# Three full-attention heads first in an encoder's attention stage, with queries loaded in token halves

## The chip, the cores and the metric

The kernel runs on one core of a Trainium2 chip. The core has a matrix engine (PE, with its weight loads shown as PEld), a vector engine (DVE), a scalar engine for pointwise functions (ACT), a second elementwise engine (POOL) and SP, which here only issues transfers. The metric is the device time of one execution in microseconds (us). Before the change it is 2045.96 us, the median of 3 runs (2044.32 to 2046.07).

## The reference

The model is a trunk of four residual layers over 1024 tokens of width 1024, all in float32: attention, MLP, spatial gating, MLP, then a final norm. The change touches the attention layer alone:

```
proj = rmsnorm(x) @ w_in                     # q, k, v of both groups in one projection
qa, ka, va, qb, kb, vb = split(proj)         # 8 query heads and 2 key heads in each group, 64 wide
qa, ka = rope(qa), rope(ka)
oa = window_attention(qa, ka, va, sink)      # group A: keys at most 128 tokens away, and a sink logit
qb, kb = rope(rmsnorm(qb)), rope(rmsnorm(kb))
ob = softmax(qb kb^T / 8) vb                 # group B: all 1024 keys
x = x + concat(oa, ob) @ w_out
```

A banded head (letter a) needs the scores of some 3 of 8 key blocks for each query block; an unbanded head (letter b) needs all of them. Both subtract the row maximum before the exponential.

## The kernel before, in words

Numbers are kept accurate by splitting each operand into a high and a low part, so that most products are three matmuls (`mm3`). The weights are split by ACT and DVE (a few by POOL) ahead of use, in the order of a list (`items`, `ahead`).

**The projections.** The attention layer begins with three of them. The first gives k and v. The second (`lin` with `evac_qb`) gives the queries of the b heads, the third (`lin` with `evac_qa`) those of the a heads. Each `lin` runs over two halves of 512 tokens; in a half it holds four PSUM banks (of 8 in all, `psp`) and goes through eight steps k of 12 matmuls. After each step it calls a hook, if there is one, and `tick()`, which moves every waiting `chain` on by one `yield`. At the end of a half, `rotate` reads two banks at a time: four DVE operations, two POOL operations, and later, in its chain, a norm (b heads and keys), a split and a store of the rotated queries to DRAM (`qs`). Only then is `ready[key, half]` set.

**The heads.** All 16 heads run in the order of the string at L538, "bbaababababababa". `load_head` (L561) reads a head's queries back from DRAM into R1 (high part, twice) and R2 (low part in its lower 64 partitions), three transfers on SP's queue for all 1024 tokens. `load_k` does the same for the keys of a key head and sets a constant with a memset on POOL. `mx_units` gives the work on the row maxima: 16 units for a b head, each one matmul over 512 keys and one DVE reduction out of PSUM (L614); 8 units for an a head (L598). Four query blocks on, `bcast` turns the maxima into a row of R2. For the first two heads this is done with four small matmuls (tile bc) and a DVE copy (L640), for all others through DRAM: a transpose on DVE and two transfers (tile md).

`st_units` gives the score units. In a b head each of 16 units is two matmuls (st), an exponential and a cast on ACT (`exps_b`, L660 and L663), and a subtraction for the low part on POOL or DVE (L665; DVE does five of the first ten, then one in eight). The product with the values (`av`, three matmuls for each unit) is held back by six units (`LAG`). `finish_head` normalises two heads of a kind at a time.

**The order around the change.** The loop over heads at L811 issues a unit of scores, then as many maxima of the heads to come as its goal asks for, then an av that is six units old, then a `tick()`. The goal of head n is all maxima of heads up to n + 1 and 0.6 of those of head n + 2. Before the loop, `qa_hook` (L800) loads the first two b heads in step 1 of the second half of the third projection and issues 20 of their 32 maxima in steps 3 to 7. The program's order is a priority: an instruction whose buffer is not free can be placed behind others when the kernel is built. On the chip each engine then works in its fixed order. The attention stage is followed by the output projection (`out_proj`), which takes the last av units along.

The large buffers are 44 blocks (`blkp`) that weights, rotated queries, R1, R2, keys and the outputs of the exponentials share.

Of the kernel before, what the change touches and what calls it, by code (L numbers as in the profile page):

```python
# [10 lines left out]
ALU = mybir.AluOpType  # L11
# [4 lines left out]
T = 1024  # L16
KT = D // P
HN = 512
# [14 lines left out]
def tile_kernel(ctx: ExitStack, tc: tile.TileContext, I, out, upto=99, dbg=None):  # L33
    nc = tc.nc
    pe, act, dve, pool, sp = nc.tensor, nc.scalar, nc.vector, nc.gpsimd, nc.sync
# [11 lines left out]
    def nm(s):  # L47
        uid[0] += 1
        return f"{s}_{uid[0]}"

    def blk(s, dt=F32R):
        return blkp.tile([P, 2, HN], dt, tag="blk", name=nm(s))
# [13 lines left out]
    def f(ap):  # L66
        return ap.bitcast(F32)
# [202 lines left out]
    def lin(rhs, evac, spare=1, swap=False, hook=None, run=True):  # L270


        g = gi[0]
        gi[0] += 1
        for half in range(2):
            acc = [ps("lin") for _ in range(4)]
            for k in range(KT):
                w = wt(g, k)
                r = rhs(k, half)
                for m in range(4):  # L280
                    ls = slice(m * P, (m + 1) * P)
                    if swap:
                        mm3(acc[m], r, w, ls, k == 0, k == KT - 1)
                    else:
                        mm3(acc[m], w, r, ls, k == 0, k == KT - 1)
                if run and k == 1:
                    ahead(base[g] + 4 + spare)
                if run and half == 1 and k % 2 == 1:
                    ahead(base[g] + 4 + spare + (k + 1) // 2)
                if hook is not None:  # L290
                    hook(half, k)
                tick()
            for m in range(4):
                evac(m, half, acc[m])
# [72 lines left out]
    h = {}  # L367
# [30 lines left out]
    def table(name):  # L398
        t = blk("tab", F32)
        sp.dma_start(t, I[name].rearrange("p (h t) -> p h t", h=2))  # L400
        return t

    rst = {}
# [18 lines left out]
    ready = {}  # L422

    def rotate(key, half, p1, p2, C, S, c1=None, c2=None, late=0):


        de, w1, w2 = blk("de", F32), tr("w1"), tr("w2")
        for o, p_, c, t in ((w1, p2, c2, S), (de[:, 0], p1, c1, C), (w2, p1, c1, S), (de[:, 1], p2, c2, C)):
            if c is None:
                dve.tensor_tensor(o, p_, t, op=ALU.mult)  # L430
            else:
                dve.scalar_tensor_tensor(o, p_, c, t, op0=ALU.mult, op1=ALU.mult)
        if c1 is not None:
            s1, s2 = tr("s1"), tr("s2")
            act.activation(s1, p1, AF.Square)
            act.activation(s2, p2, AF.Square)
            pool.tensor_tensor(s1, s1, s2, op=ALU.add)
        pool.tensor_tensor(de[:, 0], de[:, 0], w1, op=ALU.subtract)
        pool.tensor_tensor(de[:, 1], de[:, 1], w2, op=ALU.add)

        def chain():
            for _ in range(1 + late):
                yield 1
            if c1 is not None:
                yield 1
                s = ps("hss")
                mm(s, blk32, s1, True, True)
                yield 1
                y0, a, q = tr("hy"), tr("ha"), tr("hq")

                dve.scalar_tensor_tensor(a, s, 1.0 / 64.0, evb[:, half], op0=ALU.mult, op1=ALU.add)
                act.activation(y0, a, AF.Ln)
                act.activation(y0, y0, AF.Exp, scale=-0.5)
                act.activation(q, y0, AF.Square)
                yield 1
                newton(y0, q, a, 1.0, a)
                if key == "k":
                    act.copy(a[0:64], rst[half][0:64])
                for i in range(2):
                    dve.tensor_tensor(de[:, i], de[:, i], a, op=ALU.mult)  # L460
            yield 1
            for i in range(2):
                q = blk("qh")
                split(q, de[:, i])
                sp.dma_start(qs[key][:, :, :, i, half * HN : (half + 1) * HN].rearrange("a j r t -> (j r) a t"), f(q))
            ready[key, half] = True

        chains.append(chain())
# [4 lines left out]
    for half in range(2):  # L473
# [27 lines left out]
        for tb in range(4):  # L501
            sc = rc[:, tb : tb + 1]
            for kv in range(4):
                src = vp[tb // 2][:, tb % 2, kv * 64 : (kv + 1) * 64]
                hi = v1[kv][:, half * 4 + tb, 0:64]
# [13 lines left out]
    pend = {}  # L519
# [3 lines left out]
        if m % 2 == 1:  # L523
            rotate(f"b{m // 2}", half, pend[m - 1], pend[m], bc_[:, half], bs_[:, half], col(C_QN1), col(C_QN2), m // 2)

    lin(lambda k, half: h[k, half], evac_qb)
    ac, as_ = table("tac"), table("tas")
    for half in range(2):
        dve.tensor_tensor(ac[:, half], ac[:, half], rst[half], op=ALU.mult)
        dve.tensor_tensor(as_[:, half], as_[:, half], rst[half], op=ALU.mult)  # L530

    def evac_qa(m, half, p_):
        pend[m] = p_
        if m % 2 == 1:
            rotate(f"a{m // 2}", half, pend[m - 1], pend[m], ac[:, half], as_[:, half])


    heads, seen = [], {"a": 0, "b": 0}  # L538
    for c in "bbaababababababa":
        heads.append((c, seen[c]))  # L540
        seen[c] += 1
    k1, k2 = {}, {}
    R1, R2 = {}, {}
# [6 lines left out]
    def load_k(kv):  # L550
        a = blk("k1")
        b = blk("k2")
        hi, lo = (qs["k"][part, kv].rearrange("r n t -> (r n) t") for part in range(2))
        sp.dma_start(f(a[0:64].rearrange("p a b -> p (a b)")), hi)
        sp.dma_start(f(a[64:128].rearrange("p a b -> p (a b)")), lo)
        sp.dma_start(f(b[0:64].rearrange("p a b -> p (a b)")), hi)
        pool.memset(f(b[64:128]), -1.0 / 64.0)
        k1[kv] = a.rearrange("p a b -> p (a b)")
        k2[kv] = b.rearrange("p a b -> p (a b)")

    def load_head(n):  # L561
        hd = heads[n]
        kv = kv_of(hd)
        if kv not in k1:
            load_k(kv)
        key = f"{hd[0]}{hd[1] // 4}"
        assert all((q, half) in ready for q in (key, "k") for half in range(2))
        hi, lo = (qs[key][part, hd[1] % 4].rearrange("r n t -> (r n) t") for part in range(2))
        a, b = blk("r1"), blk("r2")
        a = a.rearrange("p a b -> p (a b)")  # L570
        b = b.rearrange("p a b -> p (a b)")
        sp.dma_start(f(a[0:64]), hi)
        sp.dma_start(f(a[64:128]), hi)
        sp.dma_start(f(b[0:64]), lo)
        R1[n], R2[n] = a, b

    md = drp.tile([16, 2, 32 * P], F32, tag="md", name="md")

# [42 lines left out]

    def bcast(n, half, m4):
        r2 = R2[n][64:128, half * HN : (half + 1) * HN]
        if n > 1:

            t = smp.tile([P, 32], F32, tag="m4", name=nm("mt"))
            dve.transpose(t, f(m4))
            yield 1
            sp.dma_start(md[n, half].rearrange("(a b i) -> b a i", a=32, b=4), t)
            for _ in range(3):  # L630
                yield 1
            sp.dma_start(f(r2), md[n, half, 0:HN].partition_broadcast(64))
            shifted.add((n, half))
            return
        for _ in range(2):
            yield 1
        p_ = ps("bc")
        for i in range(4):
            mm(p_[:, i * P : (i + 1) * P], m4[:, i : i + 1].to_broadcast([P, P]), ident, i == 0, i == 3)
        dve.tensor_copy(r2, p_[64:128])  # L640
        shifted.add((n, half))
# [135 lines left out]
    avq = []  # L777
    LAG = 6
    loaded = [0]
    mxq = []  # L780
    mxn = [0, 0]

    def load_to(n):
        while loaded[0] < min(n, 16):
            load_head(loaded[0])
            loaded[0] += 1

    def n_mx(n):
        return sum(8 if hd[0] == "a" else 16 for hd in heads[: max(n, 0)])

    def mx_to(count):

        while mxn[1] < min(count, n_mx(16)):
            if not mxq:
                mxq.extend(mx_units(mxn[0]))
                mxn[0] += 1
            mxq.pop(0)()
            mxn[1] += 1

    def qa_hook(half, k):  # L800
        if half == 1:
            if k == 1:
                load_to(2)
            if k >= 3:
                mx_to((k - 3 + 1) * 4)

    lin(lambda k, half: h[k, half], evac_qa, run=False, hook=qa_hook)
    h.clear()
# [2 lines left out]
    for n in range(16):  # L811
        if n > 0:
            load_to(n + 3)
        units = st_units(n)
        start, goal = mxn[1], n_mx(n + 2) + int((n_mx(n + 3) - n_mx(n + 2)) * 0.6)
        if n == 0:
            goal = n_mx(2)
        for i, u in enumerate(units):
            avs = u()
            mx_to(start + -(-(goal - start) * (i + 1) // len(units)))  # L820
            avq.append(avs)
            if len(avq) > LAG:
                for a in avq.pop(0):
                    a()
            tick()
        if n >= 13:
            ahead(base[3] + (n - 12))
# [579 lines left out]
```

## Time and profile before

| | us |
|---|---|
| median of 3 runs | 2045.96 |
| profiled execution, own time | 2044.68 |
| its span, first to last instruction | 2042.9 |
| PE busy | 2007.8 (98%) |
| DVE busy | 1402.2 (69%) |
| ACT busy | 982.4 (48%) |
| POOL busy | 591.3 (29%) |

Times in the views are us from the start of the span; 1.78 us of the execution's own time lie outside the span. [...] A row of a timeline gives start, duration, engine, line, operation, tiles and shape, the count of merged instructions and, in brackets, the engine's idle time before it and what ended that. A row of groups gives line, engine, operation, tiles, shapes and count, then busy time and mean ns, then idle time before and its releasers. All matmuls have one line (L72), so they are told apart by tile. Matmuls are pipelined: one is shown as 389 ns long while the next begins much earlier, so that short gaps do not show as idle time.

### The profile page before, as it was taken

The numbers are of one execution on the slowest core, as the hardware profiler recorded it, in microseconds if no ns is written. First come the engines' busy times: TensorE is split into PE (matmuls) and PEld (weight loads), VectorE is DVE, ScalarE is ACT, GpSimd is POOL, SyncE is SP. The second block draws the span as 40 slices with busy tenths as digits, with TensorE's granted clock in tenths as the row PEclk, the third lists the DMA queues.
The fourth block names the chain that finished last, engine by engine and source line by source line (L and its number), as shares of the span: only waits on it lengthen the run. The fifth ranks groups of instructions, "written<-read, shape, count | busy, mean of one in ns | idle before, by whom it ended". The sixth has DMA issues, their size and how long they took to land.

```text
span 2042.9 us, 27046 instructions
## 1 busy us (share of the span) xinstructions
PE 2007.8 (98%) x9038; PEld 1653.3 (81%) x9038; DVE 1402.2 (69%) x2281; ACT 982.4 (48%) x1822; POOL 591.3 (29%) x460
## 2 busy tenths in 40 slices
PE   8998999999999999999999999999999999999998
PEld 7786777778788888888888888888788888888886
DVE  6677867745886666856797445555976667836976
ACT  5526779873543333444454434433533333544443
POOL 5535557543142222100102126332232223000113
PEclk9999999999999999999999999999999999999999
DMA  5463242245054444848464210432254445856443
GB/s 172 139 191 94 65 114 57 57 135 167 36 177 149 160 149 162 295 162 314 131 215 145 78 57 11 145 119 98 88 179 146 150 159 206 300 210 208 160 134 124
DMA packets 213244, 299.05 MB, mean 146 GB/s; under 512 B 23792, under 2 KB 92912, under 8 KB 213104
## 3 DMA queue, kind: packets, MB, share of 16 engines
q1 hardware_dynamic: 213104, 297.32, 43.9%
q8 instruction: 71, 1.16, 0.2%
q14 instruction: 69, 0.57, 0.1%
HBM read 210.80 MB, written 86.44 MB: 145 GB/s over the span
## 4 chain that ended last, share of the span: by engine, by line
PE 82%; DVE 7%; ACT 5%; issue 3%; POOL 1%; DMA 1%; DVEq 0%; ACTq 0%; SPq 0%; POOLq 0%
PE up L72 27%; PE lin L72 17%; PE dy L72 17%; PE dx L72 13%; PE av L72 2%; PE st L72 2%; PE vp L72 1%; ACT pe L660 1%; PE kp L72 1%; ACT pp L663 1%; PE mx L72 1%; DVE w L145 1%; DVE mb L614 1%; DVE o L712 1%; PE dz L72 1%
## 5 line engine op out<-in xcount | busy, mean ns | idle before, releaser
L72 PE MATMUL up<-h,w 128*128 128x512 f32 x1536 | 363.2, 389 | 1.0 <-ACT w L144 0.6
L72 PE MATMUL dy<-w,w 128*128 128x512 f32 x1488 | 353.8, 389 | 0.0
L72 PEld LDWEIGHTS up<-h,w 128*128 128x128 f32 x1536 | 288.1, 188 | 61.8 <-ACT w L144 1.0
L72 PEld LDWEIGHTS dy<-w,w 128*128 128x128 f32 x1488 | 279.3, 188 | 58.4 <-ACT w L144 0.2
L313 POOL TENSOR_TENSOR ss<-ss,sq 128x512 f32<-128x512 f32 x69 | 105.9, 1536 | 653.7 <-ACT sq L311 556.3
L72 PE MATMUL dx<-w,w 128*128 128x512 f32 x1152 | 276.7, 389 | 0.0
L72 PE MATMUL up<-w,w 128*128 128x512 f32 x1152 | 276.7, 390 | 0.0
L72 PEld LDWEIGHTS up<-w,w 128*128 128x128 f32 x1152 | 216.3, 188 | 45.7 <-ACT h L863 0.5
L72 PEld LDWEIGHTS dx<-w,w 128*128 128x128 f32 x1152 | 216.3, 188 | 44.8
L144 ACT CAST w<-wr 128x512 fp32r<-128x512 f32 x288 | 167.6, 620 | 142.0 <-DVE wr L177 36.3
L145 DVE TENSOR_TENSOR w<-wr,w 128x512 fp32r<-128x512 f32 x288 | 200.9, 707 | 22.6 <-ACT w L144 18.5
L72 PE MATMUL lin<-h,w 128*128 128x512 f32 x768 | 180.8, 393 | 0.3 <-ACT mixl L1231 0.3
L984 POOL TENSOR_TENSOR t<-ua,ub 128x512 f32<-128x512 f32 x32 | 44.6, 1394 | 448.8 <-ACT ua L931 427.3
L72 PEld LDWEIGHTS lin<-h,w 128*128 128x128 f32 x768 | 143.4, 188 | 32.2 <-issue 2.4
L145 DVE TENSOR_TENSOR w<-ur,w 128x512 fp32r<-128x512 f32 x224 | 158.4, 717 | 5.8 <-ACT w L144 5.7
L665 POOL TENSOR_TENSOR pp<-pe,pp 128x512 fp32r<-128x512 f32 x107 | 140.9, 1338 | 73.1 <-ACT pp L663 48.6
L144 ACT CAST w<-ur 128x512 fp32r<-128x512 f32 x224 | 135.9, 620 | 42.9 <-DVE w L145 21.6
L145 DVE TENSOR_TENSOR w<-ws,w 128x512 fp32r<-128x512 f32 x128 | 94.9, 741 | 66.9 <-ACT w L144 66.3
L72 PE MATMUL st<-r,k 128*128 128x512 f32 (+2 forms) x384 | 130.3, 405 | 5.3 <-DVE mb L614 2.4
L144 ACT CAST w<-ws 128x512 fp32r<-128x512 f32 x128 | 79.4, 620 | 110.0 <-DVE ws L224 75.2
L931 ACT ACTIVATE ua<-ua 128x512 f32<-128x512 f32 x64 | 40.5, 633 | 168.9 <-DVE ua L930 168.7
L72 PE MATMUL av<-pp,v 128*128 128x512 f32 x384 | 110.4, 399 | 5.3 <-DVE mb L614 2.9
(195 smaller groups left out, 3012.5 us busy)
## 6 DMA issues: line engine op xcount, KB each, us to landing
ur<-ucd SPq DMA_DIRECT2D x224, 256.0 KB
wr<-in_w SPq DMA_DIRECT2D x256, 128.0 KB
ucd<-t SPq DMA_DIRECT2D x128, 256.0 KB
wr<-in_w SPq DMA_DIRECT2D x128, 256.0 KB
ucd<-ub SPq DMA_DIRECT2D x64, 256.0 KB
x<-in_xT SPq DMA_DIRECT2D x32, 256.0 KB
xmd<-x SPq DMA_DIRECT2D x32, 256.0 KB
ucd<-ua SPq DMA_DIRECT2D x32, 256.0 KB
```

The costliest lines, as they stand in the source:

```text
L72: last_mm[0] = pe.matmul(o, l, r, start=start, stop=stop, **kw)
L144: act.copy(w[:, 0], src)
L145: dve.tensor_tensor(w[:, 1], src, f(w[:, 0]), op=ALU.subtract)
L313: pool.tensor_tensor(acc, acc, t, op=ALU.add)
L614: dve.tensor_reduce(M[n][:, tb, kh : kh + 1], p_, axis=AX.X, op=ALU.max)
L660: act.activation(e, p_, AF.Exp, scale=0.125)
L663: act.copy(pp[:, 0], e)
L665: lo.tensor_tensor(pp[:, 1], e, f(pp[:, 0]), op=ALU.subtract)
L712: dve.tensor_tensor(out_, out_, y, op=ALU.mult)
L931: act.activation(dst, dst, AF.Square)
L984: pool.tensor_tensor(t3, ua[:, 1], ub[:, 1], op=ALU.subtract)
```

## The change

Three things move. The order of heads becomes "bbbaabababababaa". The keys of the first b heads are loaded at step 1 of the second half of the second projection, and the queries of the first three b heads are loaded in two token halves, each as soon as its half is stored. In the third projection the hook now issues 8 maxima in steps 4 to 7 of the first half, 24 more in steps 3 to 7 of the second (so all 32 of heads 0 and 1), and six score units of head 0 in steps 2 to 7. In the loop, head 0 has 10 score units left and takes the 16 maxima of the third b head along; head 1 takes its maxima (of the first a head) in its last nine units; a head followed by two a heads takes all maxima of the second of them. The third b head's maxima also go through the small matmuls instead of DRAM.

```
-    for c in "bbaababababababa":
+    for c in "bbbaabababababaa":
...
+    def early_keys(half, k):
+        if half == 1 and k == 1:
+            load_k(2)
+    lin(lambda k, half: h[k, half], evac_qb, hook=early_keys)
...
+        cs = slice(0, T) if part is None else slice(part * HN, (part + 1) * HN)
+        sp.dma_start(f(R1[n][0:64, cs]), hi[:, cs])
+        sp.dma_start(f(R1[n][64:128, cs]), hi[:, cs])
+        sp.dma_start(f(R2[n][0:64, cs]), lo[:, cs])
...
-        if n > 1:
+        if n > 2:
...
     def qa_hook(half, k):
-        if half == 1:
-            if k == 1:
-                load_to(2)
-            if k >= 3:
-                mx_to((k - 3 + 1) * 4)
+        for part in range(2):
+            if ("b0", part) in ready and part not in came:
+                came.append(part)
+                for n in range(3):
+                    load_head(n, part)
+                loaded[0] = 3
+        if half == 0 and k >= 4:
+            mx_to((k - 3) * 2)
+        if half == 1 and k >= 3:
+            mx_to(min(8 + (k - 2) * 5, n_mx(2)))
+        if half == 1 and k >= 2:
+            if k == 2:
+                first.extend(st_units(0))
+            avq.append(first.pop(0)())
...
-        units = st_units(n)
-        start, goal = mxn[1], n_mx(n + 2) + int((n_mx(n + 3) - n_mx(n + 2)) * 0.6)
+        units = st_units(n) if n else first
+        start, goal = mxn[1], n_mx(n + 2) + int((n_mx(n + 3) - n_mx(n + 2)) * (1.0 if next_two(n) == "aa" else 0.6))
         if n == 0:
-            goal = n_mx(2)
+            goal = n_mx(3)
         for i, u in enumerate(units):
             avs = u()
-            mx_to(start + -(-(goal - start) * (i + 1) // len(units)))
+            late = 7 if n == 1 else 0
+            mx_to(start + -(-(goal - start) * max(i + 1 - late, 0) // (len(units) - late)))
```

## Rows read from the trace of the kernel before

**Rows 1.** Stretches: the attention stage's start, and the rest of it.
```profile
157.50:190.00 32.50, 26.81 (x103) 19.41 (x104) 24.75 (x38) 20.32 (x39) 17.78 (x14) 0.95 0.50 138
190.00:430.00 240.00, 230.62 (x1060) 185.02 (x1058) 176.46 (x377) 201.56 (x384) 147.75 (x113) 1.00 0.28 73
```

**Rows 2.** Timeline of PE, from the projection's last matmuls to the second head.
```profile
156.39 1.07 PE L72 MATMUL mx<-k,r 128*128 128x512 f32 x4
...
167.65 5.06 PE L72 MATMUL av<-pp,v 128*128 128x512 f32 x14 [0.95 <-DVE mb L614]
173.72 1.65 PE L72 MATMUL av<-pp,v 128*128 128x512 f32 x6 [1.00 <-DVE pp L665]
175.21 0.56 PE L72 MATMUL bc<-ident,m 128*128 128x128 f32 x4
...
189.57 0.50 PE L72 MATMUL av<-pp,v 128*128 128x512 f32 x1 [1.37 <-POOL pp L665]
189.91 0.28 PE L72 MATMUL mx<-k,r 128*128 128x256 f32 x1
```

**Rows 3.** The chain that ended last, in the third projection: start, us, what.
```profile
119.77 22.03 PE lin L72 x97
```

**Rows 4.** Groups by shape, PE, from 157.46 to 189.9.
```profile
L72 PE MATMUL av<-pp,v 128*128 128x512 f32 x48 | 14.4, 440 | 3.4 <-POOL pp L665 1.4 <-DVE pp L665 1.0 <-DVE mb L614 0.9
L72 PE MATMUL st<-r,k 128*128 128x512 f32 x34 | 10.6, 407 | 1.6 <-DVE w L430 0.8 <-DVE mb L614 0.6
L72 PE MATMUL mx<-k,r 128*128 128x512 f32 x13 | 5.4, 416 | 0.7 <-DVE r L640 0.7
L72 PE MATMUL bc<-ident,m 128*128 128x128 f32 x8 | 1.2, 274 | 0.1
```

**Rows 5.** Stretches of 2 us with the lowest granted clock.
```profile
168.00:170.00 2.00, 2.00 (x7) 1.63 (x6) 2.00 (x3) 1.97 (x5) 1.28 (x2) 0.61 0.00 0
170.00:172.00 2.00, 2.00 (x6) 1.54 (x6) 2.00 (x3) 0.50 (x1) 0.71 (x1) 0.54 0.00 0
```

**Rows 6.** Timeline of DVE, five places.
```profile
142.06 2.48 DVE L614 TENSOR_REDUCE mb<-mx 128x1 f32<-128x512 f32 x4 [6.22 <-PE mx L72]
...
163.93 1.50 DVE L665 TENSOR_TENSOR pp<-pe,pp 128x512 fp32r<-128x512 f32 x1
...
166.19 0.69 DVE L665 TENSOR_TENSOR pp<-pe,pp 128x512 fp32r<-128x512 f32 x1
...
182.51 0.16 DVE L617 TENSOR_REDUCE m<-mb 128x4 fp32r<-128x8 f32 x1
190.22 0.48 DVE L598 CUSTOM_DVE_ANT_0 mj<-mx,maskq,sink 128x256 f32<-128x256 f32 x1 [7.56 <-PE mx L72]
```

**Rows 7.** Groups by shape, DVE, from 142 to 182.7.
```profile
L614 DVE TENSOR_REDUCE mb<-mx 128x1 f32<-128x512 f32 x32 | 20.4, 681 | 7.4 <-PE mx L72 7.3
L665 DVE TENSOR_TENSOR pp<-pe,pp 128x512 fp32r<-128x512 f32 x7 | 6.8, 969 | 0.0
L430 DVE TENSOR_TENSOR w<-lin,tab 128x512 f32<-128x512 f32 x4 | 2.7, 680 | 0.0
```

**Rows 8.** Timeline of ACT: the first exponential.
```profile
158.86 0.60 ACT L660 ACTIVATE pe<-st 128x512 f32<-128x512 f32 x1 [19.72 <-PE st L72]
```

**Rows 9.** Timeline of SP's queue: stores and loads of queries.
```profile
127.05 4.39 SPq L465 DMA_DIRECT2D qs_b<-qh  x4
...
134.41 0.47 SPq L572 DMA_DIRECT2D r<-qs_b  x1
...
145.17 29.19 SPq L465 DMA_DIRECT2D qs_a<-qh  x8
...
177.78 0.53 SPq L572 DMA_DIRECT2D r<-qs_a  x1
```

**Rows 10.** Timeline of PE: the last head's scores.
```profile
423.34 0.44 PE L72 MATMUL st<-r,k 128*128 128x384 f32 x1 [1.42 <-DMA r<-md]
```

**Rows 11.** Groups by shape, POOL, from 190 to 430.
```profile
L665 POOL TENSOR_TENSOR pp<-pe,pp 128x512 fp32r<-128x512 f32 x98 | 129.1, 1340 | 61.3 <-ACT pp L663 36.8 <-PE st L72 12.4 <-DMA r<-md 10.0
```

More of the change, by code (lines that the diff above doesn't have):

```diff
@@ L524, in evac_qb @@
             rotate(f"b{m // 2}", half, pend[m - 1], pend[m], bc_[:, half], bs_[:, half], col(C_QN1), col(C_QN2), m // 2)
[L526 to L535, printed above, removed]
     heads, seen = [], {"a": 0, "b": 0}
-    for c in "bbaababababababa":
+    for c in "bbbaabababababaa":
         heads.append((c, seen[c]))
@@ L559, in load_k, with evac_qa, load_head @@
         k2[kv] = b.rearrange("p a b -> p (a b)")
-    def load_head(n):
+    def early_keys(half, k):
+        if half == 1 and k == 1:
+            load_k(2)
+    lin(lambda k, half: h[k, half], evac_qb, hook=early_keys)
+    ac, as_ = table("tac"), table("tas")
+    for half in range(2):
+        dve.tensor_tensor(ac[:, half], ac[:, half], rst[half], op=ALU.mult)
+        dve.tensor_tensor(as_[:, half], as_[:, half], rst[half], op=ALU.mult)
+    def evac_qa(m, half, p_):
+        pend[m] = p_
+        if m % 2 == 1:
+            rotate(f"a{m // 2}", half, pend[m - 1], pend[m], ac[:, half], as_[:, half])
+    def load_head(n, part=None):
         hd = heads[n]
@@ L566, in load_head @@
         key = f"{hd[0]}{hd[1] // 4}"
-        assert all((q, half) in ready for q in (key, "k") for half in range(2))
+        assert all((q, half) in ready for q in (key, "k") for half in range(2) if q == "k" or part in (None, half))
         hi, lo = (qs[key][part, hd[1] % 4].rearrange("r n t -> (r n) t") for part in range(2))
[L569 to L575, printed above, removed]
+        if n not in R1:
+            R1[n], R2[n] = (blk(name).rearrange("p a b -> p (a b)") for name in ("r1", "r2"))
+        cs = slice(0, T) if part is None else slice(part * HN, (part + 1) * HN)
+        sp.dma_start(f(R1[n][0:64, cs]), hi[:, cs])
+        sp.dma_start(f(R1[n][64:128, cs]), hi[:, cs])
+        sp.dma_start(f(R2[n][0:64, cs]), lo[:, cs])
     md = drp.tile([16, 2, 32 * P], F32, tag="md", name="md")
@@ L798, in mx_to, with next_two @@
             mxn[1] += 1
+    first, came = [], []
+    def next_two(n):
+        return "".join(hd[0] for hd in heads[n + 1 : n + 3])
     def qa_hook(half, k):
-        if half == 1:
-            if k == 1:
-                load_to(2)
-            if k >= 3:
-                mx_to((k - 3 + 1) * 4)
+        for part in range(2):
[12 more added lines that the diff above has]
+            avq.append(first.pop(0)())
     lin(lambda k, half: h[k, half], evac_qa, run=False, hook=qa_hook)
```

## The prediction

> **What bounds the kernel now.** I went from the stretches to PE's timeline, then to the other engines' timelines at the places where PE waits. From 190 to 430 us PE is shown busy for 230.62 of 240 us, so 9.4 us idle or 3.9%; from 157.5 to 190, the first head and the way into the second, for 26.81 of 32.5, so 5.7 us idle or 17.5% [rows 1]. The reader should see that PE bounds the attention stage as a whole, and that its beginning is the exception.
>
> Shown idle time is too small, as a spaced matmul is still drawn 389 ns long. The pitch says more. The third projection's last maxima end at 156.39 + 1.07 = 157.46 us; the first maximum of a banded head starts at 189.91 [rows 2]. In a dense run 97 matmuls take 22.03 us, 0.227 us each [rows 3]. Between the two times PE runs 48 av, 34 st and 13 mx matmuls, 95 x 0.227 = 21.6 us, and 8 bc matmuls in 1.2 us [rows 4]: 22.8 us of work in 32.45. So 9.7 us are lost, 5.7 of them shown as idle. The named waits are for DVE (0.95 and 1.00) and POOL (1.37) [rows 2], and for DVE's rotation of the projection's banks (0.8) and its copy of maxima into R2 (0.7) [rows 4]. [...]
>
> Why does it lose here? DVE stands still for 6.22 us until the first maximum at 142.06, works almost without a gap until the last b maximum's reduction near 182.51, and stands still again for 7.56 us until the first a maximum at 190.22 [rows 6]. In the busy stretch lie 32 reductions (20.4 us), seven low parts (6.8) and the rotation of the last half [rows 7]. ACT waits 19.72 us for its first score, until 158.86 [rows 8]. The second gap on DVE exists because the a queries are late: SP's stores of them last from 145.17 to 174.36, and their loads begin at 177.78 [rows 9]. So the start is a DVE pile with a hole on either side.
>
> **The change part by part.**
>
> *Six scores and 12 more maxima in the third projection.* They cost PE the same there as later: 12 st and 12 mx matmuls, 24 x 0.227 = 5.4 us by [rows 3], which the projection gets longer and head 0 shorter. ACT's 12 operations fall into its 19.72 us hole [rows 8]: nothing. What they bring is that at the projection's end all maxima of heads 0 and 1 are out and six units of av (18 matmuls, 4.1 us) need no new bank, while DVE rotates the last half (eight operations of 0.68 us, by the form in [rows 7], 5.4 us) and holds the projection's four banks. In the kernel before, PE had nothing of the kind there.
>
> *The third b head first.* DVE's second hole [rows 6] is filled with the 16 maxima of b2, whose queries need no a store; a0's come in the last nine units of head 1, when its loads [rows 9] have landed. The reductions are moved, not added: 16 x 0.68 = 10.9 us of DVE that the two holes (6.22 + 7.56 = 13.8 us) can just take.
>
> *What the three together give.* The lower bound is shown idle time above the ordinary share: 5.7 - 0.039 x 32.5 = 4.4 us. The upper bound is all that is lost by the pitch, 9.7. Ordinary losses of later heads stay in the start too, so I take the middle: 7.0 us. If nothing of it is gained, because DVE is as late as before, the bound is 0; a rival below goes under that.
>
> *Earlier loads in halves.* Nine more transfers on SP (18 instead of 9 for three heads), and the first nine are issued once the first half of b0 is stored, the others behind its second half. The stores of both pairs' second half start at 127.05 and take 4.39 us; a load's issue takes some 0.5 [rows 9]. So nine loads are out about 5 us behind the b0 stores, some 134 us, before the maxima that need them (step 3 of the second half; before, the loads from 134.41 served the maxima reduced at 142.06). Behind them on SP wait the stores of b1's second half, which nobody needs before head 4, and then the a stores. The early key load needs stores that were done in the second projection; its memset on POOL stands earlier beside idle time. Cost nothing; no row shows a load that PE waits for in this stretch; were one late, PE would stand for what is missing, up to a batch of four reductions (2.48 us [rows 6]), and below 0 there is nothing to gain.
>
> *New traffic in the projection.* Eight maxima (5.4 us of DVE) now precede the rotation of the first half, and DVE must free four banks before the second half has all of its own. Below: 0, since the PE order is built around banks that are not free, and DVE's 6.22 us hole lies just behind. Above: the whole 5.4. In the dense second half of before, 20 maxima stood among the matmuls without a named wait; by that I take 1.0.
>
> *Third head's maxima by matmul.* Eight more bc matmuls, two groups of 0.56 us [rows 2]: 1.1 us on PE, and two DVE copies in place of two transposes. Taken in full; the lower end is 0, if they fall into gaps.
>
> *The end.* The last a head's scores wait 1.42 us for the transfer of maxima that were finished just before [rows 10]. Now an a head of eight units stands between the last maxima and this use, so I take 1.4 off; bounds 0 and 1.4.
>
> *The middle.* The same heads in another order, three b in a row first, then a a, and a a at the end. Zero, with -3 and +3 as bounds: up to a third of the 9.4 us of idle time from 190 to 430 [rows 1].
>
> Sum: 7.0 - 1.0 - 1.1 + 1.4 = 6.3 us. The profiled execution took 2044.68 (span 2042.9), so 2038.4; the median of the runs stands 1.28 above it, so 2045.96 - 6.3 = **2039.7 us**.
>
> [...] One low part on DVE takes 0.69 us (166.19) and another 1.50 (163.93) [rows 6]; POOL is at work on the a rotation or its own low parts in this stretch. [...]
>
> **The rivals.**
>
> *The wait moves into the three b heads.* Heads 1 and 2 in a row bring 28 low parts to POOL, 28 x 1.34 = 37.5 us [rows 11], against 32 units of 5 matmuls on PE, 36.3 us; before, an a head stood between most b heads. For it: the wait of 1.37 for POOL at 189.57 [rows 2]. Against it: POOL's low parts mostly waited for ACT (36.8 of 61.3 us idle) [rows 11], and six units of lag cover one late part. If each of the three b heads ended with such a wait and its dead time, 3 x 1.4, the gain is 2.1: 2043.9.
>
> *The edit does not do what it says.* If the shared blocks are not free while 16 blocks of the projection's input and 8 of weights are alive, R1 and R2 come late, the 8 first maxima slide into the second half, and 32 reductions (20.4 us [rows 7]) compete there with rotation and low parts; the hole before 142.06 stays. I give it what the end and the second hole's half bring, 1.4 + 2: 2042.6 without the bc cost, 2043.7 with it.
>
> *DVE is the bound, and it becomes slower.* Head 0 now carries 16 reductions instead of 12 in fewer units, on top of the rotation. If the first hole is not used, DVE is 10.9 us further behind at head 0's end, and PE, which works in a fixed order with maxima between scores, stands behind it. Of the 10.9 us PE uses 16 x 0.227 = 3.6 for the matmuls themselves, which it saves later; the rest, 7.3, is loss, less the 1.4 at the end, with the 1.1 for bc: 7.0 slower, 2053; if half of it is absorbed in head 1's seven units without maxima, 3.4 slower, about 2049.3. It decides once DVE ends the projection more than one rotation (5.4 us) behind PE. Against it: a dense stretch of before had 20 reductions in steps 3 to 7, now 24, and the holes are large enough by sum.
>
> **How the numbers follow.** The forecast's case 0.62 (its own range 2035 to 2042.2, from the bounds 9.7 and 4.4, with the middle's part); waits in the b heads 0.18; edit without effect 0.08; DVE-bound 0.12. A change under 0.2%, 4.1 us, can't be told from none. The forecast's case is faster in about 0.57 of its 0.62, the two next in 0.09 of their 0.26; the last is slower in 0.07 of its 0.12. So faster 0.66, same 0.24, slower 0.10. For 8 in 10 the range takes in the forecast's case with a gain in the middle, and the two next: 2033.5 to 2047.
>
> **What would show it.** Right: DVE has no gap over 3 us between the middle of the third projection and the first a maximum; the granted clock stays 1.00 to the second head; ACT's first exponential comes some 15 us earlier; the projection ends about 5 to 7 us later than 157.46, and the b1 scores start before 185; the wait of 1.42 us at the last head is gone. Wrong: PE waits for DVE's rotation or for a load inside the projection (the 1.0 is too small), for POOL's low parts in heads 1 and 2 (first rival), or still runs at the lower clock behind the projection (third). The output projection and all behind it must only shift.

## The result, and the profile after

The changed kernel takes 2060.17 us, the median of 4 runs (2058.44 to 2060.29), where the kernel before took 2046.01 on the same chip: a ratio of 1.0068 (95% interval 1.0056 to 1.008), 14.2 us slower. The forecast was 2039.7, with 2033.5 to 2047 as the range. The profiled execution took 2058.44 (span 2056.7). All of the loss lies in the attention stage: the first matmul of the layer behind it (tile up) starts at 522.10 us before and at 535.76 after, 13.7 of the span's 13.8. The changed kernel's lines stand 3 or 4 further down: the reductions L614 are L617 in its views, L617 (the gathering into m) is L620, the copy L640 is L643, the exponential L660 is L663, the low parts L665 are L668.

By stretches, DVE has filled up, PE has not. A row gives the stretch, its length, the busy time and the number of instructions of PE, PEld, DVE, ACT and POOL, then the granted PE clock as a share of full speed, the busy share of the DMA engines and GB/s:

```profile
157.50:190.00 32.50, 24.47 (x105) 17.60 (x104) 31.12 (x48) 13.32 (x24) 13.56 (x10) 0.91 0.21 75
190.00:430.00 240.00, 228.11 (x1010) 181.03 (x1010) 170.09 (x357) 194.74 (x368) 151.27 (x114) 0.97 0.27 68
...
184.00:186.00 2.00, 0.00 (x0) 0.00 (x0) 2.00 (x2) 0.00 (x0) 1.73 (x2) 0.50 1.00 373
...
183.90:194.20 10.30, 4.81 (x13) 3.99 (x14) 9.65 (x16) 2.60 (x5) 3.20 (x4) 0.50 1.03 302
238.50:245.40 6.90, 6.14 (x16) 4.99 (x17) 3.66 (x15) 5.43 (x11) 4.92 (x5) 0.51 0.26 72
358.00:361.50 3.50, 3.37 (x10) 2.81 (x11) 1.60 (x6) 3.45 (x8) 3.50 (x4) 0.51 0.03 5
```

DVE is busy for 31.12 of 32.5 us, before for 24.75 [rows 1]; PE for 24.47 instead of 26.81. In the row from 184 to 186 us PE, PEld and ACT do nothing while DVE and POOL work. PE's timeline says what stands there, and where it began:

```profile
133.74 1.65 PE L72 MATMUL lin<-h,w 128*128 128x512 f32 x6 [1.66 <-DVE mb L617]
136.73 4.37 PE L72 MATMUL lin<-h,w 128*128 128x512 f32 x18 [1.34 <-DVE mb L617]
...
165.66 1.07 PE L72 MATMUL mx<-k,r 128*128 128x512 f32 x4
...
182.20 0.50 PE L72 MATMUL mx<-k,r 128*128 128x512 f32 x1 [0.45 <-ACT pe L663]
189.39 1.11 PE L72 MATMUL bc<-ident,m 128*128 128x128 f32 x4 [6.69 <-DVE m L620]
190.31 1.16 PE L72 MATMUL st<-r,k 128*128 128x512 f32 x2
...
239.25 1.65 PE L72 MATMUL av<-pp,v 128*128 128x512 f32 x3 [2.65 <-DVE ma L601]
...
358.13 1.22 PE L72 MATMUL st<-r,k 128*128 128x512 f32 x2 [1.42 <-DVE mb L617]
```

Between the halves of the projection PE waits 1.66 + 1.34 = 3.0 us for DVE; the projection's last maxima end at 165.66 + 1.07 = 166.7 instead of 157.46 [rows 2], 9.3 later, of which the 24 matmuls moved into it are 5.4. Then PE waits 6.69 us, and the matmuls behind the wait run at half the full clock (granted clock 0.50 in the row from 183.90 to 194.20; it fell during the wait, from 1.00 until 183.50 to 0.50 from 184.00 on): the two st at 190.31 take 1.16 where the two at 195.83, with the clock at 1.00 again, take 0.62. Counted in this timeline, head 0's scores end at 195.1 (182.9 before), the fifth head's at 264.7 (250.7).

The clock is down twice more in the stage, to 0.51, at the waits for DVE of 2.65 us before 239.25 and of 1.42 before 358.13. In the three rows PE is busy for 4.81 + 6.14 + 3.37 = 14.3 us at about half clock. The kernel before has one such stretch, 3.50 us around [rows 5]:

```profile
168.40:171.90 3.50, 3.50 (x10) 2.72 (x10) 3.50 (x5) 2.07 (x4) 1.59 (x2) 0.51 0.00 0
```

With the clock at half, half of that time is taken as lost, an estimate from these rows: 7.2 us against 1.8, so some 5.4 us of the loss. The rest is PE's idle time. From 119 us to the start of tile up, after and before:

```profile
119.00:535.76 416.76, 393.29 (x1737) 312.88 (x1736) 288.51 (x531) 265.48 (x495) 197.99 (x147) 0.98 0.33 96
```

```profile
119.00:522.10 403.10, 387.41 (x1730) 310.58 (x1729) 279.92 (x530) 265.17 (x495) 194.67 (x148) 1.00 0.36 104
```

PE is idle for 23.5 us instead of 15.7, 7.8 more. With the 5.4 of the clock that makes 13.2 of the 13.7 (one profiled execution of each kernel).

PE waits for m, the reduction at 189.19 that gathers eight maxima. DVE's timeline shows what is in front of it:

```profile
140.25 0.68 DVE L430 TENSOR_TENSOR de<-lin,tab 128x512 f32<-128x512 f32 x1
...
146.13 0.69 DVE L668 TENSOR_TENSOR pp<-pe,pp 128x512 fp32r<-128x512 f32 x1 [3.75 <-ACT pp L666]
146.74 2.49 DVE L299 TENSOR_TENSOR qh<-de,qh 128x512 fp32r<-128x512 f32 x4
...
172.88 0.68 DVE L430 TENSOR_TENSOR de<-lin,tab 128x512 f32<-128x512 f32 x1
...
180.04 0.69 DVE L617 TENSOR_REDUCE mb<-mx 128x1 f32<-128x512 f32 x1
180.65 5.62 DVE L299 TENSOR_TENSOR qh<-de,qh 128x512 fp32r<-128x512 f32 x4
186.20 0.68 DVE L668 TENSOR_TENSOR pp<-pe,pp 128x512 fp32r<-128x512 f32 x1
186.80 2.47 DVE L617 TENSOR_REDUCE mb<-mx 128x1 f32<-128x512 f32 x4
189.19 0.14 DVE L620 TENSOR_REDUCE m<-mb 128x4 fp32r<-128x8 f32 x1
```

DVE works without a gap to speak of, one thing behind the other: rotation of the last half, low parts and the third head's reductions in turn, then the four low parts of the rotated a queries (L299), a low part of the scores, four reductions, m. The four a low parts take 5.62 us; the four of the other half, at 146.74, took 2.49. POOL's timeline around the long ones:

```profile
180.49 1.29 POOL L668 TENSOR_TENSOR pp<-pe,pp 128x512 fp32r<-128x512 f32 x1 [3.43 <-ACT pp L666]
182.73 2.99 POOL L668 TENSOR_TENSOR pp<-pe,pp 128x512 fp32r<-128x512 f32 x2 [0.95 <-ACT pp L666]
```

POOL runs low parts of its own beside three quarters of that time; beside the four at 146.74 it ran nothing. (Of the scores' first ten low parts DVE takes seven by the code, not five: numbers 1, 2, 3, 5, 7, 9 and 10. They are the seven of [rows 7].) The chain that ended last names DVE as the bound of this stretch (start, us, what):

```profile
166.23 2.48 DVE mb L617 x4
...
180.73 5.54 DVE qh L299 x4
...
186.88 2.39 DVE mb L617 x4
189.39 1.11 PE bc L72 x4
```

ACT does begin 14 us earlier than in [rows 8], and the a queries are later than in [rows 9], as SP's queue shows: their loads begin at 189.03, not 177.78.

```profile
144.85 0.60 ACT L663 ACTIVATE pe<-st 128x512 f32<-128x512 f32 x1 [11.95 <-PE st L72]
```

```profile
111.49 0.46 SPq L576 DMA_DIRECT2D r<-qs_b  x1
...
131.38 0.45 SPq L576 DMA_DIRECT2D r<-qs_b  x1
...
147.46 39.20 SPq L465 DMA_DIRECT2D qs_a<-qh  x8
189.03 0.47 SPq L576 DMA_DIRECT2D r<-qs_a  x1
```

The wait of [rows 10] is gone: no wait of PE between 415 and 450 us names a transfer.

### The profile page after: what moved, and what is told of

The parts are those of the page before. It is cut to its first block, busy times and chain, and to the rows that moved or that the text cites. A ratio compares the mean times of both kernels' runs of the same rounds, so it can differ in the third digit from the quotient of the medians.

```text
span 2056.7 us, 27049 instructions
## 1 busy us (share of the span) xinstructions
PE 2013.5 (98%) x9046; PEld 1654.6 (80%) x9046; DVE 1410.1 (69%) x2281; ACT 982.8 (48%) x1822; POOL 596.3 (29%) x460
## 3 DMA queue, kind: packets, MB, share of 16 engines
q8 instruction: 71, 1.16, 0.2%
## 4 chain that ended last, share of the span: by engine, by line
PE 83%; DVE 8%; ACT 4%; issue 2%; POOL 2%; DMA 1%; DVEq 0%; SPq 0%; ACTq 0%; POOLq 0%
PE up L72 27%; PE dy L72 16%; PE lin L72 16%; PE dx L72 13%; PE av L72 3%; PE st L72 2%; PE mx L72 1%; PE vp L72 1%; PE kp L72 1%; DVE mb L617 1%; DVE w L145 1%; POOL pp L668 1%; DVE qh L299 1%; PE dz L72 1%; PE mix L72 0%
## 5 line engine op out<-in xcount | busy, mean ns | idle before, releaser
L668 POOL TENSOR_TENSOR pp<-pe,pp 128x512 fp32r<-128x512 f32 x107 | 145.7, 1386 | 106.7 <-ACT pp L666 62.5
```

The source lines that it names most:

```text
L668: lo.tensor_tensor(pp[:, 1], e, f(pp[:, 0]), op=ALU.subtract)
```

## The experiments

Each cost below is the kernel's median less that of the kernel before, measured beside it (2045.87 to 2046.25); the changed kernel stands at +14.2. Intervals are of the ratio to the kernel before. A difference between the changed kernel and a variant of it carries both intervals, together some 4 us each way.

**The 6.7 us wait.** Theory A: a small matmul's place in PE's order is at fault. Theory B: DVE is late, whatever PE waits for. Theory C: POOL's low parts are late.

*The third head's maxima through DRAM again* (from the changed kernel):

```
-        if n > 2:
+        if n > 1:
```

> The changed kernel (2060.2 us), with one line put back: the maxima of the third b head go through DRAM again, not through the eight bc matmuls. Theory A (the loss at 182 to 194 us is PE's fixed order: the bc matmuls of head 2 stand in front of head 0's and head 1's work and wait 6.7 us for reductions that DVE reaches only after four low parts of a queries): the 6.7 us wait goes, so do about 2 us at the lower clock behind it and 0.8 us of bc work, 2050 to 2052. Theory B (DVE is late as a whole, whatever PE waits for): the wait turns up at another instruction for DVE in the same stretch, 2057 to 2060.

Measured: +10.5 (2056.76; 1.0037 to 1.007). PE's timeline:

```profile
180.57 0.98 PE L72 MATMUL mx<-k,r 128*128 128x512 f32 x2 [0.41 <-ACT pe L663]
186.26 1.22 PE L72 MATMUL st<-r,k 128*128 128x512 f32 x2 [4.71 <-DVE mb L617]
```

Without the bc matmuls PE waits 4.7 us at the same place for a reduction behind the same pile. The medians differ by 3.7, which is what the small matmuls were worth, though no more than the two intervals together; A falls as the whole cause, B holds.

*The third head's maxima not in head 0, but with the first a head's in head 1*:

```
-            goal = n_mx(3)
+            goal = n_mx(2)
...
-            late = 7 if n == 1 else 0
+            late = 0
```

> The changed kernel, but head 0 takes no maxima of the third b head along; head 1 takes them over all its 16 units. Same order of heads, same bc matmuls. Theory A: the reductions then fall into DVE's free time of head 1 (it is idle for some 20 us in all between 196 and 232), no bc stands in front of the a queries' low parts: 2050 to 2053. Theory B: DVE has 16 reductions less in its full stretch, which also helps, but PE loses it again in head 1: 2054 to 2058.

Measured: +6.2 (2052.48; 1.0019 to 1.0046). Taking the 16 reductions out of head 0 gives back 7.9, more than half of the loss. The edit also lets head 1 take the first a head's maxima without holding them back, but the gain stands before that: head 0's scores end at 180.2 instead of 195.1 (16 maxima matmuls, 3.6 us, are moved out of it), head 1's at 212.2 instead of 216.5. What the lifted hold does in head 1 was not tried by itself here. PE still waits 2.59 us for a low part on DVE at 183.22.

*The low parts of the a queries on POOL* (from the changed kernel):

```
-                split(q, de[:, i])
+                split(q, de[:, i], pool if key[0] == "a" else None)
```

> The changed kernel (2060.2 us), with the eight low parts of the rotated a queries on POOL instead of DVE. Theory B (DVE is the engine that is late in the start): DVE loses 2.5 us in the projection and 5.6 us in front of the third head's reductions, so the 6.7 us wait of PE shrinks by 4 to 6 us: 2054 to 2057. Theory A (PE's order alone): no less than 2059, since POOL takes as long.

Measured: +9.4 (2055.57; 1.0036 to 1.0066), so 4.8 back, little more than the intervals. PE's wait for m shrinks by 3.85 us:

```profile
184.74 0.63 PE L72 MATMUL bc<-ident,m 128*128 128x128 f32 x4 [2.84 <-DVE m L620]
```

*Every fourth low part on DVE instead of every eighth, for the first 48* (C):

```
-        lo = dve if cnt[0] % 8 == 2 or ...
+        lo = dve if cnt[0] % (4 if cnt[0] <= 48 else 8) == 2 or ...
```

> The changed kernel, with one low part in four instead of one in eight on DVE in the first three heads. Theory C (POOL is the bound of heads 1 and 2, 28 low parts of 1.4 to 1.5 us without a gap): some four parts less on POOL, 4 to 6 us less of its time there, of which PE gets 2 to 4: 2056 to 2058. If POOL isn't the bound or DVE's extra parts only block it: 2060 or more.

Measured: +16.2 (2062.37; 1.0069 to 1.0099). Relief for POOL and load for DVE make it no better; C is not supported here.

*Both loads off DVE*, the later maxima and the a low parts on POOL (the two edits above together):

> The changed kernel with two loads on DVE taken out of head 0's stretch at once: the third head's maxima only in head 1, and the a queries' low parts on POOL. Alone they brought 7.7 and 4.6 us. If both act through the same pile on DVE, together they bring less than the sum, 8 to 10 us: 2050 to 2052, the order's 3.9 us above the kernel before. If they act apart: 2048.

Measured: +5.2 (2051.11; 1.0015 to 1.0035). Together 9.0 back, alone 7.9 and 4.8, sum 12.7: less than the sum, as two parts of one pile would give, but the difference of 3.7 is within the intervals.

**The order of the heads.** *The new order alone* (from the kernel before):

```
-    for c in "bbaababababababa":
+    for c in "bbbaabababababaa":
...
-        ... int((n_mx(n + 3) - n_mx(n + 2)) * 0.6)
+        ... int((n_mx(n + 3) - n_mx(n + 2)) * (1.0 if <two a heads next> else 0.6))
```

> The kernel before (2046.0 us), with the new order of heads alone (and the rule that a head followed by two a heads takes all maxima of the second). Nothing is loaded early and nothing of the heads stands in the first half of the third projection. Theory C (three b heads in a row make POOL the bound: in the changed kernel it runs from 204 to 248 us with almost no gap): slower than before by 4 to 6 us, 2050 to 2052. Theory A and B: the order by itself costs nothing, 2044 to 2047.

Measured: +3.9 (2050.11; 1.0011 to 1.003), where the prediction had a middle of 0 ± 3 and 1.4 off at the end.

*The new front, the old end* ("bbbaaabababababa"):

> The new order's front alone (bbbaaabababababa): three b heads first, then three a heads, and the old alternation to the end, with the rest as in the kernel before (2046.1 us). If the order's cost of 3.9 us is made in the first five heads, as the traces have it (the fifth head's scores end at 256.3 us against 251.4), it is here too: 2049 to 2051. If the two a heads at the end make it: 2045 to 2047.

Measured: +3.05 (2048.92; 1.0009 to 1.0027). The cost is at the front. PE's timeline of this kernel, where the third b head and the first a head meet:

```profile
230.23 0.96 PE L72 MATMUL av<-pp,v 128*128 128x512 f32 x3 [1.67 <-DVE ma L598]
234.19 0.97 PE L72 MATMUL av<-pp,v 128*128 128x512 f32 x3 [0.35 <-POOL pp L665]
235.44 0.96 PE L72 MATMUL av<-pp,v 128*128 128x512 f32 x3 [0.28 <-POOL pp L665]
...
239.16 0.50 PE L72 MATMUL av<-pp,v 128*128 128x512 f32 x1 [0.28 <-POOL pp L665]
```

PE first waits for a banded head's maximum, then takes the last av of the b head at the pace of POOL's low parts (1.24 us apart). With the two rows left out, 0.28 each, these waits make 3.1 us. The new order alone shows the same waits; the kernel before has no wait over 0.76 us between 190 and 260. From head 0's last score to the fifth head's last (182.7 to 255.8) PE is idle for 5.9 us here and for 2.7 in the kernel before (182.9 to 250.7; the expectation's 251.4 counts one row too far); from there to the last head's it is 8.0 and 8.1. So in this run the front's 3 us are these waits.

*Is it POOL?* Every second low part of the second and third b head is left out, with the order and, as a control, in the kernel before:

```
+        if 16 < cnt[0] <= 48 and cnt[0] % 2:
+            return pp, 0
...
-            mm(o, a, pp[:, 1, c0 : c0 + w_], False, last)
+            mm(o, a, pp[:, low, c0 : c0 + w_], False, last)
```

> The new order alone (2050.1 us, 3.9 above the kernel before), with every second low part of its second and third b head left out (the third av matmul reads the high part again, so PE has the same work). Theory C (POOL is the bound in three b heads in a row): most of the order's 3.9 us is gone, 2046 to 2047. Rival (the order costs by other waits, on ACT's casts or DVE): no gain over 1 us, 2049 to 2051. Its control is the next kernel.

> The control: the kernel before (2046.2 us) with the same low parts left out (second and third b head of its own order, with two a heads between them). Theory C: POOL has slack here, at most 1 us faster, 2045 to 2046. Rival: it gains as much as the new order does from it.

Measured: the order -0.15 (2045.98; 0.9989 to 1.0008), so 4.0 less than with all low parts; the control -3.2 (2042.90; 0.9978 to 0.9996). Leaving them out helps both kernels alike, and the order is still 3.1 behind. POOL's low parts cost PE something in either order, but the order's cost does not go with them: of the waits at 230 to 239 us only one of 0.34 is left here, and a gap stays. It lies elsewhere: between the fifth head's last score and the last head's, PE is idle for 10.1 us with the order and for 8.1 in the control.

**The early part.** *Early keys, halves, 32 maxima and six scores, in the old order*: from the changed kernel, the old string, two heads instead of three loaded in the hook, the old goals.

> The early part alone, in the old order of heads: early keys, the queries of two b heads in halves, all their maxima and six score units in the third projection. Theory A: the projection's own cost stays (PE waits 3.0 us for DVE between its two halves), but the start behind it improves by the 7 us that I had predicted: 2041 to 2043. Theory B: DVE is no earlier, since its work is the same, and the 3 us come on top: 2047 to 2050.

Measured: +1.4 (2047.65; 1.0 to 1.0018): a small loss or none, and no gain. The waits of PE:

```profile
134.04 1.66 PE L72 MATMUL lin<-h,w 128*128 128x512 f32 x6 [1.66 <-DVE mb L617]
137.03 4.41 PE L72 MATMUL lin<-h,w 128*128 128x512 f32 x18 [1.33 <-DVE mb L617]
...
183.06 0.50 PE L72 MATMUL av<-pp,v 128*128 128x512 f32 x1 [2.58 <-DVE pp L668]
189.06 0.50 PE L72 MATMUL av<-pp,v 128*128 128x512 f32 x1 [1.13 <-POOL pp L668]
192.09 0.55 PE L72 MATMUL mx<-k,r 128*128 128x256 f32 x1 [2.53 <-DMA r<-qs_a]
```

The early part does bring something, and loses it at once: head 0's scores end at 180.0 us, 2.9 earlier than before, head 1's at 208.8, 3.2 later (205.6). Between them lie the three last waits above, for a low part on DVE, one on POOL and the load of the a queries, which the longer projection makes late; behind them the clock is down:

```profile
191.50:195.00 3.50, 2.91 (x8) 2.55 (x9) 1.12 (x4) 0.89 (x2) 0.00 (x0) 0.51 1.03 222
```

*Without the scores in the projection* (from the run above; head 0 makes all 16 units itself):

```
-        if half == 1 and k >= 2:
-            if k == 2:
-                first.extend(st_units(0))
-            avq.append(first.pop(0)())
```

> The early part alone in the old order, all 32 maxima in the third projection but no early score: the six score units stand in head 0 again. If the early scores bring what was expected of them (av work that PE can do while DVE rotates): 3 to 5 us slower than with them, 2051 to 2053. If they bring nothing, as the start's end doesn't move with them: 2046 to 2048.

Measured: +1.7 (2047.53; 1.0 to 1.0019). In the end the six early scores neither bring nor cost anything that shows, though ACT starts 20.5 us earlier with them (145.19 instead of 165.72): head 0's scores end 4.6 us earlier with them, head 1's 2.7 later.

*Without maxima in the first half*: all 32 in steps 1 to 7 of the second, three scores from step 5.

> The early part alone in the old order (2047.7 us), but no maximum in the first half of the third projection: all 32 in steps 1 to 7 of the second half, and only three early score units (steps 5 to 7), since the maxima are there later. Theory D (the eight maxima in the first half are what makes PE wait 3.0 us for DVE between the halves, because DVE reduces them before it frees the four banks): that wait goes, three early scores less cost 1 at most, 2044 to 2046. Rival (DVE's pile is only moved on into the second half and to the start of head 0): 2047 to 2050.

Measured: +6.1 (2052.32; 1.0021 to 1.0049). The 3.0 us between the halves are gone, but PE waits 3.59 us for a reduction at 140.90 and 2.73 for a low part at 187.07. The pile has moved and grown; the 3.0 were not to be had by this.

*The same with the a low parts on POOL and the first a head's maxima late in head 1*:

> Old order of heads, early loads in halves, all 32 maxima in the second half, three early scores, low parts of the a queries on POOL, and the first a head's maxima in the last nine units of head 1. If DVE's pile and the late a queries are the two causes that hold the early part back (PE waits 2.6 us for a low part on DVE and 2.5 us for the load of the first a head in the run with the early part alone): 2039 to 2043, better than both kernels. If PE loses the time to POOL in their place: 2046 to 2049.

Measured: +3.3 (2049.50; 1.0009 to 1.0028), above both ranges and 2.8 below the run before it. The rival's mechanism is there: PE waits 1.45 us at 173.62 and 3.25 at 182.41 for low parts on POOL.

*The early part with the a low parts on POOL*:

> The early part alone in the old order (2047.7 us) with the low parts of the a queries on POOL. Theory B (DVE's pile, here before the low part that PE waits 2.6 us for): 2042 to 2045, as the same move brought 3.0 to the kernel before and 4.6 to the changed one. If the early part has its own limit besides DVE: 2046 or more.

Measured: +2.9 (2048.76; 1.0006 to 1.0025), no better than without. POOL's timeline, then PE's:

```profile
175.63 1.75 POOL L668 TENSOR_TENSOR pp<-pe,pp 128x512 fp32r<-128x512 f32 x1
177.33 5.91 POOL L299 TENSOR_TENSOR qh<-de,qh 128x512 fp32r<-128x512 f32 x4
183.21 6.20 POOL L668 TENSOR_TENSOR pp<-pe,pp 128x512 fp32r<-128x512 f32 x5
```

```profile
184.52 4.68 PE L72 MATMUL av<-pp,v 128*128 128x512 f32 x12 [2.81 <-POOL pp L668]
...
191.81 0.50 PE L72 MATMUL av<-pp,v 128*128 128x512 f32 x1 [1.38 <-POOL pp L668]
193.18 0.36 PE L72 MATMUL mx<-k,r 128*128 128x256 f32 x1 [0.87 <-DMA r<-qs_a]
```

The longer projection brings the a queries' rotation later, so their low parts now meet the scores' low parts on POOL, and PE waits for those instead.

**A version that beats both.** *The kernel before, with the a low parts on POOL and nothing else*:

> The kernel before with the eight low parts of the rotated a queries on POOL instead of DVE. Theory B (DVE's pile sets the start, in the kernel before too): DVE has 5.8 us less to do between 144 and 173 us, PE's waits for it in the start shrink, 2041 to 2044. Rival (POOL, which then has four parts more between the rotation and its first low parts of the exponentials, takes over the wait): 2046 to 2049.

Measured: -3.0 (2043.12; ratio 0.9987, 0.9978 to 0.9996), the fastest of the kernels that compute the whole. POOL's timeline, DVE's, and the stretch of the start:

```profile
165.72 5.88 POOL L299 TENSOR_TENSOR qh<-de,qh 128x512 fp32r<-128x512 f32 x4 [0.45 <-ACT qh L298]
```

```profile
188.32 0.48 DVE L598 CUSTOM_DVE_ANT_0 mj<-mx,maskq,sink 128x256 f32<-128x256 f32 x1 [5.81 <-PE mx L72]
```

Here the four stand ahead of POOL's low parts of the scores; the first a maximum comes 1.9 us earlier than in [rows 6], and PE is busy for 28.74 us of the start instead of 26.81 [rows 1]:

```profile
157.50:190.00 32.50, 28.74 (x118) 21.25 (x117) 24.27 (x39) 22.37 (x43) 23.77 (x18) 0.95 0.50 138
```

PE's 1.37 us for POOL at 189.57 [rows 2] is gone. The profiled executions differ by only 1.0 us, as the one of before (2044.68) is among the quicker ones of its kernel; the 3.0 rests on the medians.

*The same, and the first a head's maxima in the last nine units of head 1*:

```
-            mx_to(start + -(-(goal - start) * (i + 1) // len(units)))
+            late = 7 if n == 1 else 0
+            mx_to(start + -(-(goal - start) * max(i + 1 - late, 0) // (len(units) - late)))
```

> The same, and the first a head's maxima only in the last nine units of head 1, so that PE does not come to them before the a queries are loaded (in the kernel before, DVE stands for 7.56 us until the first of them). If late a queries hold the start: another 1 to 2 us, 2040 to 2043. If not: as the run before it or up to 1 us slower.

Measured: +1.2 (2047.32; 0.9993 to 1.0012). That is 4.2 more than without the hold, measured beside it, where at most 1 was expected: in this kernel, holding these maxima back costs about 4 us. PE waits 1.87 us for ACT at 193.11, where the kernel without the hold has no wait.

## Why the prediction was wrong

**The reading of the bound was right, its use was not.** PE lost time at the start because of DVE's pile. The forecast filled DVE's holes with moved reductions, by sums: 13.8 us of holes for 10.9 us of work. But a hole is not free for any work. The 6.22 us before 142.06 were a wait for PE's maxima [rows 6]; after the change DVE still stood 3.75 us before 146.13, now for ACT, and the reductions of the third head went to head 0, behind the rotation, the scores' and the a queries' low parts: the last of PE's maxima before its wait ended at 182.20 + 0.50 = 182.7, and the four reductions just ahead of m came at 186.80, behind the 5.62 us of low parts. The step "what the three together give", 7.0 us of gain with 4.4 and 9.7 as ends, gave none: the early part alone wins 2.9 us by the end of head 0, loses 6.1 in head 1 and ends at +1.4, and the third head's maxima in head 0 cost 7.9. The forecast also had no term for the clock behind a wait that is moved or new; by the estimate above that alone is some 5.4 us.

**New traffic in the projection**, 1.0 with 0 to 5.4 as ends, was 3.0 in named waits. It was argued from 20 maxima in the second half that cost nothing; those stood after the rotation, while the new ones precede the release of four banks. The range held, the value was too small.

**Third head's maxima by matmul**, 1.1 for eight matmuls, was 3.7 by the medians. The price of the matmuls was right; missing was that they put into PE's order an instruction that waits for the end of a DVE pile (6.69 us for m). The prediction asked what is queued behind a wait for the loads on SP, and not here.

**The middle**, 0 ± 3, and **the end**, 1.4 off: the order together costs 3.9, and 3.05 with the front alone. The wait at the last head went as foretold, yet the old end shows no gain or loss beside it that these intervals can tell. Why three b heads in front cost PE some 3 us is open in part: the waits are shown (a banded maximum, then POOL's pace) and make up the front's cost, but what puts them there is not, and with half of POOL's low parts they went and a gap of 3.1 stayed.

**The account.** 3.9 for the order, 1.4 for the early part and 7.9 for the third head's maxima (measured inside the changed kernel, with the hold lifted too, so parts overlap) make 13.2 of 14.2. The traces divide the same loss into 7.8 us of idle time and some 5.4 of lower clock. The sum behind the forecast's own range is uneven: 9.7 in the place of 7.0 gives 2037.0 and 4.4 gives 2042.3; the 2035 takes some of the middle's 3 us in, the 2042.2 none. It changes nothing here.

**The rival that came true** is "DVE is the bound", with a chance of 0.12 and 2053. Its mechanism is the chain shown above; its price was 7 us short. It left out the order (3.9) and the matmuls at half speed (some 5.4 us more than before); these overlap, as the fall of the clock at 358 has its like in the new order alone: the three av at 350.51, behind a wait of 1.43, take 1.49 us there, as the three at 359.15 take 1.48 in the changed kernel with the clock at 0.51, where three at 355.86 take 0.85. The argument against it, that holes are large enough by sum, is what failed. Its point of decision, DVE ending the projection more than 5.4 us behind PE, told nothing: DVE's last rotation ends at 172.88 + 0.68 = 173.6, 6.8 behind PE, but before it was already 162.74 + 0.68 = 163.4, 6.0 behind 157.46.

**The longer low parts.** Four low parts took 5.62 us beside POOL's and 2.49 without, so by estimate some 3.1 of the 6.7 us wait. The rotation at 172.88, which takes one input from PSUM, keeps its 0.68 us beside 1.29 us of POOL's (172.82). The two low parts of the scores that the prediction names differ in the same way: the one of 1.50 at 163.93 runs beside POOL's rotation (1.29 us from 163.59), the one of 0.69 at 166.19 while POOL is idle (2.54 us before 167.42). The forecast's sum has no term for these 0.8 us, and the a queries' low parts, where the price was paid, are not in its account. Other causes of the longer operations were not tried one by one.

**The signs.** DVE was to have no gap over 3 us between the middle of the projection and the first a maximum; it has 3.75 before 146.13 and 5.58 before 204.96. Right were the first exponential 14 us earlier and the last head's wait gone. Wrong were the clock (0.50 instead of 1.00), the projection's end (9.3 later, not 5 to 7) and head 1's scores, which start behind 195, not before 185. Of the signs listed as wrong, PE's wait for DVE inside the projection (3.0) and the third rival's, the lower clock behind the projection, were there.

## What to carry to other kernels

Idle time of an engine is not a store to be filled by sum: ask for each hole what it waited for, and for each moved instruction what stands ahead of it there. Before a cheap operation is put into the bound engine's order, look at the engine that makes its input: here four small matmuls inherited DVE's pile as a wait of 6.69 us, and 4.8 us of work behind it ran at a granted clock of 0.50. When a pile stands on one engine, look first for one step of it that an idle engine can take at that moment; here one line gave 3.0 us where the whole rearrangement cost 14.2, and the same line with the early part gave nothing (+2.9 against +1.4).

## What was not expected of the hardware

A low part on DVE (128x512, two SBUF inputs) takes 0.62 us in a run of four when POOL is idle (146.74), and 1.4 when POOL runs its own (180.65); on POOL the same four take 5.88 us, 1.47 each. So moving them costs POOL about what they cost DVE beside POOL's own. And during a wait of 6.69 us on PE the granted clock fell to 0.50 and stayed there for 4.8 us of full work behind it. It was down behind shorter waits too, of 2.65 us (6.1 us of work at 0.51) and of 1.42 (3.4 us), while the clock stayed up behind 1.37 us (189.57 in [rows 2]; granted 1.00 from 188 to 194) and 1.67 (230.23 with the new front: the three av behind it take 0.96 us, those behind the 2.65 take 1.65).
